# The w_out stage of a hybrid encoder step: norm row multiplied in as results leave PSUM, squares summed from PSUM, residual added in the last VectorE operation

## The chip, the cores and the metric

The kernel runs on one core of a Trainium2 chip. The metric is the device time of one execution in microseconds (us). Two times are told apart: the median of the timed runs, and the time of one execution that the hardware profiler recorded, from which all the rows of the profile come.

## The reference

One layer of a streaming encoder is computed for 2048 prompt rows and 128 sample rows (8 groups of 16), each row 1024 values wide, in float32. The stage that matters here is the third line: the two mixers' outputs are joined, multiplied by the 1024x1024 matrix `w_out`, normalised by the root mean square, scaled by a row of gains `norm_g[1]`, and added to the input.

```
att = rms_norm(att, g_att)                                  # 512 wide
mlstm_out = (hb * g_mlstm * sigmoid(ob))                    # 512 wide
x = x + rms_norm(concatenate([att, mlstm_out], -1) @ w_out, norm_g[1])
ffn, new_buf = conv_ffn(rms_norm(x, norm_g[2]), conv_buf, w_up, w_conv, b_conv, w_down)
x = x + rms_norm(ffn, norm_g[3])

def rms_norm(x, g):
    return x * rsqrt(mean(x * x, axis=-1, keepdims=True) + EPS) * g
```

The mean of squares is over the row before the gains are applied.

## The kernel before

The kernel is written with tiles and pools; a scheduler simulates the timeline when the kernel is built and puts each engine's instructions into an order from that. So a change in one place can move instructions on every engine near it.

The program has three large parts: the input projection with attention and mLSTM, the w_out stage, and the feed-forward part (an up projection, a short convolution, a gate, a down projection). Every matmul on large operands is done as three matmuls (`mm3`, L104 to L106) of pieces `hi` and `lo` of both factors: ScalarE makes `hi` by a cast and VectorE makes `lo` by subtracting `hi`. Splitting weights in the feed-forward part is done by L1309 (ScalarE) and L1310 (VectorE); combinations of weights are formed on VectorE in L1326.

The w_out stage is `project(tiles)` (L974 to L1040), a generator. It is advanced step by step, and between its steps other generators are advanced by a ratio of costs: at first the last attention heads (scores L394 and L395, transposes of the weights L76 into tile `pt`, their hi and lo pieces `pth` L417 and `ptl` L418, the product with the values L430 and L431 into `ot`), and from tile 8 on the first units of the feed-forward part (the rows of x are loaded as `x2r`, squared in L1095, scaled in L1099, transposed in L1107). The rows are taken in 17 tiles of 128 rows: tiles 0 to 7, then the sample tile (16), then tiles 8 to 15. For each tile:

- the joined row tile `mr` is loaded (two tiles ahead); for the next tile the attention half is normalised: a square with accumulation on ScalarE (L995), mean and inverse root on GpSimd (`rsqrt_mean`, L87 and L93), and the scaling on VectorE in L997;
- `turn_rows` transposes `mr` on TensorE (L76, PSUM tile `mT_pt`) and splits the result into the hi and lo pieces `mt` (L210 on ScalarE, L211 on VectorE). For tiles 0 to 7 this goes in two groups of four through the same PSUM buffers as the accumulators below (tag `mm`, two buffers); from the sample tile on through a larger buffer of its own (tag `big`);
- for each half `hf` of 512 columns 24 matmuls are accumulated in a PSUM tile `wo`. The half is evacuated by VectorE into `m` (L1026), and ScalarE squares it with accumulation (L1028); the squares themselves are written to a place that is free at that time and never read;
- the inverse root is formed on GpSimd (L87, L93), VectorE scales `m` by it and by the gains (L1038), GpSimd adds the residual row tile `xr` (L1039), and SyncE's queue stores the sum as `x2d` (L1040).

`m` and `xr` are the two halves of one tile `mx` (tag `wl`, two buffers); `xr` is loaded by SyncE's queue when the tile is begun (L1016). The slots of `wl` are used later for `wul`, the lo pieces of the first feed-forward weights. The gains lie in a tile of one buffer, `norm_row` (tag `grow`): row 1 is loaded ahead of the stage, and the row for the last norm of the layer takes its place after it (L98). There are 34 evacuations L1026, 34 squares L1028, and 17 each of L1038, L1039 and L1040. At the end of the kernel the last normalisation evacuates its PSUM tile with a product (L1691) and squares the same PSUM tile on ScalarE (L1692).

Of the kernel before, what the change touches and what calls it, by code (L numbers as in the profile page):

```python
# [12 lines left out]
AF = mybir.ActivationFunctionType  # L13
ALU = mybir.AluOpType
# [35 lines left out]
def hymba_step(ctx: ExitStack, tc: tile.TileContext, I: dict, O: dict):  # L50
    nc = tc.nc
# [8 lines left out]
    def ps_mm(name):  # L60
        return psum.tile([P, 512], F32, tag="mm", name=name)
# [24 lines left out]
    def mean_square(ms, ssq, n, eps=EPS):  # L86
        nc.gpsimd.tensor_scalar(ms, ssq, 1.0 / n, eps, op0=ALU.mult, op1=ALU.add)  # L87

    def rsqrt_mean(ssq, n, name, eps=EPS):
        ms = small.tile([P, 1], F32, tag="ms", name=name + "_ms")  # L90
        mean_square(ms, ssq, n, eps)
        rs = small.tile([P, 1], F32, tag="rs", name=name + "_rs")
        nc.gpsimd.tensor_tensor(rs, ms, nhalf[:, 0:1], op=ALU.pow)  # L93
        return rs
# [7 lines left out]
    def mm3(out, ah, al, bh, bl, start, stop, onto=False):  # L102

        nc.tensor.matmul(out, ah, bh, start=start, stop=False, skip_group_check=onto)  # L104
        nc.tensor.matmul(out, ah, bl, start=False, stop=False, skip_group_check=onto)  # L105
        nc.tensor.matmul(out, al, bh, start=False, stop=stop, skip_group_check=onto)  # L106
# [23 lines left out]
    def x_src(t):  # L130
        return I["x_sample"] if t == SAMPLE else I["x_prompt"][t * P:(t + 1) * P, :]
# [69 lines left out]
    def rows_to_T(hrow, chunk, j, name, bank):  # L201
        w = 4 if bank is not ps_big else KT
        for q in range(KT // w):
            pt = bank(f"{name}_pt{q}")
            for k in range(w):
                transpose(pt[:, k * P:(k + 1) * P], hrow[:, (w * q + k) * P:(w * q + k + 1) * P])
            ptv = pt.rearrange("p (k t) -> p k t", k=w)
            hv = chunk[:, 0, w * q:w * q + w, j * P:(j + 1) * P]
            lv = chunk[:, 1, w * q:w * q + w, j * P:(j + 1) * P]
            nc.scalar.copy(hv, ptv)  # L210
            nc.vector.tensor_tensor(lv, ptv, hv, op=ALU.subtract)  # L211
# [4 lines left out]
    def rows_tile(tag, shape, name, dtype=F32):  # L216
        if tag == "xr":
            return rows.tile(shape, dtype, tag="xr", name=name, bufs=2)
        return pa.tile(shape, dtype, tag=tag, name=name, bufs=1)
# [718 lines left out]
    g1 = []  # L938
# [31 lines left out]
    def drain():  # L970
        while any([p_.step() for p_ in pipes]):
            pass

    def project(tiles):  # L974

        ss = [SimpleNamespace(t=t) for t in tiles]

        def load(s):
            t = s.t
            if t == 8:  # L980
                drain()
                open_ffn()
            s.m = rows_tile("xr", [P, D], f"mr{t}")
            if t == SAMPLE:
                for b in range(DB):
                    own = bass.AP(atts[b].tensor, atts[b].offset, [[512, DS], [DS * 512 + DA, HA], [1, DA]])
                    nc.sync.dma_start(s.m[b * DS:(b + 1) * DS, 0:512].rearrange("p (h d) -> p h d", h=HA), own)
                nc.sync.dma_start(s.m[:, 512:D], mixs)
            else:
                nc.sync.dma_start(s.m, mixd[t // 4][:, t % 4, :])  # L990

        def norm(s):
            mt = wpool.tile([P, 2112], F32R, tag="wh", name=f"mt{s.t}", bufs=2)
            ssq = small.tile([P, 1], F32, tag="ssq", name=f"assq{s.t}")
            nc.scalar.activation(mt[:, :512], s.m[:, :512], AF.Square, accum_out=ssq)  # L995
            rs = rsqrt_mean(ssq, 512, f"att{s.t}")
            nc.vector.tensor_scalar(s.m[:, :512], s.m[:, :512], rs, None, op0=ALU.mult)  # L997
            s.mt = mt[:, :2 * D].rearrange("p (a k n) -> p a k n", a=2, k=KT)

        def turn_rows(s):  # L1000
            rows_to_T(s.m, s.mt, 0, f"mT{s.t}", ps_mm if s.t < 8 else ps_big)

        load(ss[0])
        norm(ss[0])
        yield 0.0, 0.3
        turn_rows(ss[0])
        load(ss[1])
        yield 0.9, 1.2
        for n_, s in enumerate(ss):
            t = s.t  # L1010
            nxt = ss[n_ + 1] if n_ + 1 < len(ss) else None
            if nxt:
                norm(nxt)
            mx = wpool.tile([P, 2112], F32, tag="wl", name=f"mx{t}", bufs=2)
            m, xr = mx[:, 0:D], mx[:, D:2 * D]
            nc.sync.dma_start(xr, x_src(t))  # L1016
            for hf in range(2):
                c = slice(hf * 512, hf * 512 + 512)
                acc = ps_mm(f"wo{t}_{hf}")
                for k in range(KT):  # L1020
                    mm3(acc, s.mt[:, 0, k, :], s.mt[:, 1, k, :], wo[k][0][:, c], wo[k][1][:, c],
                        start=(k == 0), stop=(k == KT - 1))
                    if k % 4 == 3:
                        yield 2.6, 0.5
                ssq = small.tile([P, 1], F32, tag="wssq", name=f"wssq{t}_{hf}")
                nc.vector.tensor_copy(m[:, c], acc)  # L1026
                idle = m[:, 512:D] if hf == 0 else s.mt[:, 0, 0:4, :].rearrange("p k n -> p (k n)")
                nc.scalar.activation(idle, m[:, c], AF.Square, accum_out=ssq)  # L1028
                if hf == 0:
                    ssa = ssq  # L1030
                    mean_square(ssa, ssq, D)
                    if nxt:
                        turn_rows(nxt)
                        if n_ + 2 < len(ss):
                            load(ss[n_ + 2])
                        yield 0.9, 1.2
            rs = rsqrt_mean(ssq, D, f"n1_{t}", ssa)
            nc.vector.scalar_tensor_tensor(m, m, rs, g1[0], op0=ALU.mult, op1=ALU.mult)  # L1038
            nc.gpsimd.tensor_tensor(xr, m, xr, op=ALU.add)  # L1039
            nc.sync.dma_start(x2d[t], xr)  # L1040


# [6 lines left out]
    def open_ffn():  # L1049

        p1.close()
        ffn.p3 = ctx.enter_context(tc.tile_pool(name="p3", bufs=2, reuse_waits="tile"))
        ffn.halo = ffn.p3.tile([P, 44, 2], F32, tag="halo", name="halo", bufs=1)
        nc.vector.memset(ffn.halo, 0.0)
        ffn.g2 = ffn.p3.tile([P, D], F32, tag="g2", name="g2", bufs=1)
        nc.sync.dma_start(ffn.g2, I["norm_g"][2:3, :].broadcast_to([P, D]))
        pipes[:] = [Pipe(h2_units(0, lead=6)), Pipe(iter([]))]
# [187 lines left out]
    for n_, (half, gi) in enumerate(seq):  # L1245
# [22 lines left out]
        if n_ == len(seq) - 1:  # L1268
            out = project([0, 1, 2, 3, 4, 5, 6, 7, SAMPLE, 8, 9, 10, 11, 12, 13, 14, 15])
            split = w_out_steps()  # L1270
            next(split)
            next(out)
# [194 lines left out]
    for b, tiles in enumerate(FBLOCKS):  # L1467
# [137 lines left out]
        for fi, f in enumerate(ORDERS[b]):  # L1605
# [12 lines left out]
            e, c = ec[:, 0:512], ec[:, 512:1024]  # L1618
# [193 lines left out]
        for dh in range(2):  # L1812
# [59 lines left out]
            for j in order:  # L1872
                if dh == 0:
                    half, ssq = out[j]
# [3 lines left out]
                else:  # L1878
                    half, ssq = out[j]
# [3 lines left out]
                    rs = p3.tile([P, 1], F32, tag=f"drs{j}", name=f"drs{tiles[j]}", bufs=2)  # L1883
# [104 lines left out]
```

## Time and profile before

| | |
|---|---|
| median of 3 runs | 2769.81 us (2767.66 to 2773.04) |
| profiled execution | 2768.79 us |
| its span | 2767.1 us |
| instructions | 47724 |
| TensorE busy | 2697.3 us, 97% of the span |
| VectorE busy | 1933.3 us, 70% |
| ScalarE busy | 1437.5 us, 52% |
| GpSimd busy | 674.8 us, 24% |

In the profile PE is TensorE's matmul, PEld its weight load, DVE is VectorE, ACT ScalarE, POOL GpSimd and SP SyncE, whose queue issues most transfers. `L1026` is line 1026 of the kernel. In a row of the trace, `mx<-wo` reads "written from", in square brackets stands how long the engine was idle before the instruction and what ended that, and `x17` is a count. The span runs from the first to the last recorded instruction; the time of the execution is 1.7 us longer here.

### The profile page before, as it was taken

Reading aid. Unit: us, or ns where it says so; the run is one execution under the profiler, and the core shown is the slowest. Engines: PE = TensorE matmul, PEld = TensorE weight load, DVE = VectorE, ACT = ScalarE, POOL = GpSimd, SP = SyncE. Lnnn points to the kernel's source line nnn. Section 1 sums busy time; section 2 is a strip of 40 time slices with the busy share of each in tenths; the row PEclk is TensorE's granted clock in tenths of the full one; section 3 lists DMA queues with packets and bytes.
Section 4 is the critical chain, followed back from the end, with each engine's and each line's share of the span. In section 5 each row is a group of like instructions: output and inputs, shape, how many; then the busy total and the mean of one; then the engine's idle time right before and its main releaser. Section 6 shows DMA issues by size and latency. Waiting matters only on the chain.

```text
span 2767.1 us, 47724 instructions
## 1 busy us (share of the span) xinstructions
PE 2697.3 (97%) x16422; PEld 2522.0 (91%) x16422; DVE 1933.3 (70%) x3593; ACT 1437.5 (52%) x2918; POOL 674.8 (24%) x1293
## 2 busy tenths in 40 slices
PE   8999999999999999999999999999999999999998
PEld 7899999999899998878999998789999878998976
DVE  5344455646446668766989988658888875998956
ACT  4355555635356666543555455444554665554554
POOL 1000010212100002334433322123343212556401
PEclk9999999999999999999999999999999999999999
DMA  5544355556564456345645559867886877788875
GB/s 186 156 120 137 104 164 167 160 154 213 161 183 142 137 168 197 109 165 196 231 152 188 167 179 331 296 225 203 245 239 182 252 236 242 220 263 239 253 262 178
DMA packets 329185, 539.72 MB, mean 195 GB/s; under 512 B 60354, under 2 KB 162974, under 8 KB 328814
## 3 DMA queue, kind: packets, MB, share of 16 engines
q1 hardware_dynamic: 248382, 393.82, 45.9%
q0 software_dynamic: 35632, 97.48, 11.4%
q10 hardware_dynamic: 44928, 45.37, 5.0%
q8 instruction: 129, 2.11, 0.3%
q14 instruction: 114, 0.93, 0.1%
HBM read 383.28 MB, written 162.68 MB: 197 GB/s over the span
## 4 chain that ended last, share of the span: by engine, by line
PE 51%; DVE 4%; DMA 2%; issue 1%; ACT 1%; POOL 1%; SPq 0%; DVEq 0%; POOLq 0%; ACTq 0%
PE uec L104 6%; PE uec L105 5%; PE uec L106 5%; PE dn L106 4%; PE dn L105 4%; PE dn L104 4%; PE ua L106 3%; PE ua L105 3%; PE ua L104 3%; PE dnm L105 2%; PE dnm L106 2%; PE dnm L104 2%; PE wo L106 2%; PE wo L104 2%; PE wo L105 1%
## 5 line engine op out<-in xcount | busy, mean ns | idle before, releaser
L104 PE MATMUL uec<-B,wuh 128*128 128x384 f32 (+1 forms) x720 | 236.3, 329 | 2.6 <-DVE uu L1646 2.6
L105 PE MATMUL uec<-B,wuh 128*128 128x384 f32 (+1 forms) x720 | 235.1, 327 | 0.0
L106 PE MATMUL uec<-B,wul 128*128 128x384 f32 (+1 forms) x720 | 233.7, 327 | 0.0
L1309 ACT CAST wuh<-wu 128x512 fp32r<-128x512 f32 x255 | 141.6, 618 | 107.4 <-PE uec L105 100.7
L1310 DVE TENSOR_TENSOR wul<-wu,wuh 128x512 fp32r<-128x512 f32 x255 | 165.0, 683 | 4.0 <-DMA x2d<-mx 2.8
L405 DVE CUSTOM_DVE_ANT_0 tmp<-s,nb 128x640 f32<-128x640 f32 (+4 forms) x128 | 94.3, 737 | 93.7 <-PE s L395 92.3
L104 PE MATMUL vo<-wi_h,hT 128*128 128x256 f32 x544 | 155.7, 286 | 0.6 <-DVE mt L211 0.6
L106 PE MATMUL vo<-wi_h,hT 128*128 128x256 f32 x544 | 156.2, 287 | 0.0
L105 PE MATMUL vo<-wi_l,hT 128*128 128x256 f32 x544 | 155.5, 286 | 0.0
L104 PEld LDWEIGHTS uec<-B,wuh 128*128 128x128 f32 x720 | 135.1, 188 | 6.1 <-DVE uu L1646 4.3
L105 PEld LDWEIGHTS uec<-B,wuh 128*128 128x128 f32 x720 | 135.3, 188 | 0.2
L106 PEld LDWEIGHTS uec<-B,wul 128*128 128x128 f32 x720 | 135.1, 188 | 0.0
L418 DVE TENSOR_TENSOR ptl<-pt,pth 128x640 fp32r<-128x640 f32 (+4 forms) x128 | 93.6, 737 | 57.7 <-ACT pth L417 56.7
L104 PE MATMUL qk<-hT,wi_h 128*128 128x384 f32 (+1 forms) x384 | 128.6, 335 | 5.0 <-ACT qk_st L236 3.9
L406 ACT ACTIVATE tmp<-tmp,mn 128x640 f32<-128x640 f32 (+4 forms) x128 | 97.6, 762 | 64.7 <-DVE mn L405 61.8
L1310 DVE TENSOR_TENSOR wdl<-wdr,wdh 128x512 fp32r<-128x512 f32 x198 | 125.0, 684 | 7.4 <-ACT wdh L1309 7.2
L1310 DVE TENSOR_TENSOR al<-ar,ah 128x768 fp32r<-128x768 f32 (+2 forms) x94 | 70.8, 763 | 82.1 <-ACT ah L1309 80.0
L105 PE MATMUL qb<-hT,wi_h 128*128 128x384 f32 (+1 forms) x384 | 127.9, 333 | 0.0
L105 PE MATMUL qk<-hT,wi_h 128*128 128x384 f32 (+1 forms) x384 | 127.6, 332 | 0.0
L106 PE MATMUL qk<-hT,wi_l 128*128 128x384 f32 (+1 forms) x384 | 127.3, 331 | 0.0
L106 PE MATMUL qb<-hT,wi_l 128*128 128x384 f32 (+1 forms) x384 | 127.2, 331 | 0.0
L104 PE MATMUL qb<-hT,wi_h 128*128 128x384 f32 (+1 forms) x384 | 127.2, 331 | 0.0
(448 smaller groups left out, 9404.0 us busy)
## 6 DMA issues: line engine op xcount, KB each, us to landing
wu<-in_w_up SPq DMA_DIRECT2D x220, 256.0 KB, 4.7
wu<-wsd SPq DMA_DIRECT2D x176, 256.0 KB, 4.5
wdr<-in_w_down SPq DMA_DIRECT2D x110, 256.0 KB, 5.2
wi_raw<-in_w_in SPq DMA_DIRECT2D x52, 512.0 KB, 4.0
wsd<-ws POOLq DMA_DIRECT2D x88, 256.0 KB, 3.5
wdr<-wtd SPq DMA_DIRECT2D x88, 256.0 KB, 5.1
gr<-gd SPq DMA_DIRECT2D x39, 384.0 KB, 5.9
kraw<-kTd SPq DMA_DIRECT2D x112, 128.0 KB, 3.5
```

The lines of the kernel that those rows point to most:

```text
L104: nc.tensor.matmul(out, ah, bh, start=start, stop=False, skip_group_check=onto)
L105: nc.tensor.matmul(out, ah, bl, start=False, stop=False, skip_group_check=onto)
L106: nc.tensor.matmul(out, al, bh, start=False, stop=stop, skip_group_check=onto)
L405: nc.vector.tensor_tensor_reduce(o_, s_, b_, 1.0, 3e38, ALU.add, ALU.min, accum_out=mn)
L406: nc.scalar.activation(tmp[:, :n], tmp[:, :n], AF.Exp, bias=mn, scale=-1.0, accum_out=rsum[:, i % 4, hh:hh + 1])
L418: nc.vector.tensor_tensor(s.ptl[:, sl, qc], ptv, s.pth[:, sl, qc], op=ALU.subtract)
L1309: nc.scalar.copy(h, r)
L1310: nc.vector.tensor_tensor(l, r, h, op=ALU.subtract)
```

## The change

The evacuation of each half multiplies by the gains instead of copying. The squares are taken from the PSUM accumulator, since `m` now holds the product with the gains, and the mean of squares must be taken before it. The last VectorE operation multiplies `m` by the inverse root and adds the residual row in the place of the gains, and writes into `xr`. The addition on GpSimd is gone. One line fewer makes every later line of the changed kernel one lower, so that L1310 and L1326 are there L1309 and L1325.

```
                 ssq = small.tile([P, 1], F32, tag="wssq", name=f"wssq{t}_{hf}")
-                nc.vector.tensor_copy(m[:, c], acc)
+                nc.vector.tensor_tensor(m[:, c], acc, g1[0][:, c], op=ALU.mult)
                 idle = m[:, 512:D] if hf == 0 else s.mt[:, 0, 0:4, :].rearrange("p k n -> p (k n)")
-                nc.scalar.activation(idle, m[:, c], AF.Square, accum_out=ssq)
+                nc.scalar.activation(idle, acc, AF.Square, accum_out=ssq)
...
             rs = rsqrt_mean(ssq, D, f"n1_{t}", ssa)
-            nc.vector.scalar_tensor_tensor(m, m, rs, g1[0], op0=ALU.mult, op1=ALU.mult)
-            nc.gpsimd.tensor_tensor(xr, m, xr, op=ALU.add)
+            nc.vector.scalar_tensor_tensor(xr, m, rs, xr, op0=ALU.mult, op1=ALU.add)
             nc.sync.dma_start(x2d[t], xr)
```

The order of instructions differs from before only in a stretch of each engine's queue from the w_out stage to the start of the feed-forward part; ahead of it and behind it the rows are the same. Three places are shown.

GpSimd between the end of tile 6 and the end of tile 7, before (`n_6` are the mean and inverse root of a w_out row, `att` those of the attention half of the next tile, `wssq` a sum of squares of one half):

```order
L87 TENSOR_SCALAR n_6_ms<-wssq_1_15073,wssq_0_14960 128x1
L93 TENSOR_TENSOR n_6_rs<-n_6_ms,nhalf 128x1
L87 TENSOR_SCALAR att_ms<-assq_15084 128x1
L93 TENSOR_TENSOR att_rs<-att_ms,nhalf 128x1
L1039 TENSOR_TENSOR mx_14881<-mx_14881 128x1024
L87 TENSOR_SCALAR wssq_0_15144<-wssq_0_15144 128x1
L87 TENSOR_SCALAR n_7_ms<-wssq_1_15196,wssq_0_15144 128x1
```

The same place of the same engine in the changed kernel:

```order
L87 TENSOR_SCALAR n_6_ms<-wssq_1_15067,wssq_0_14954 128x1
L93 TENSOR_TENSOR n_6_rs<-n_6_ms,nhalf 128x1
L87 TENSOR_SCALAR att_ms<-assq_15077 128x1
L93 TENSOR_TENSOR att_rs<-att_ms,nhalf 128x1
L87 TENSOR_SCALAR wssq_0_15137<-wssq_0_15137 128x1
L87 TENSOR_SCALAR n_7_ms<-wssq_1_15189,wssq_0_15137 128x1
```

The addition of 128x1024 that stood between the inverse root for the next tile's attention half and the mean of squares of the next half is gone; nothing has taken its place.

TensorE where the transposes of tile 7 stand among the last attention heads, before, with the semaphores that each instruction waits on (`mT_pt` are the two groups of transposes, `s` is a score tile):

```order
L76 MATMUL mT_pt_14964<-ident,mr_14800 128x128 [waits DMAHW6_49,DVE_49]
L76 MATMUL mT_pt_14964<-ident,mr_14800 128x128 x3
L76 MATMUL mT_pt_14971<-ident,mr_14800 128x128 [waits DVE_49]
L76 MATMUL mT_pt_14971<-ident,mr_14800 128x128 x3
L394 MATMUL s_14_14988<-kh_3_14572,qs_3_14574 128x320 [waits DVE_49]
```

The same place in the changed kernel:

```order
L76 MATMUL mT_pt_14958<-ident,mr_14795 128x128 [waits DMAHW6_49,DVE_49]
L76 MATMUL mT_pt_14958<-ident,mr_14795 128x128 x3
L76 MATMUL mT_pt_14965<-ident,mr_14795 128x128 [waits Activation_49]
L76 MATMUL mT_pt_14965<-ident,mr_14795 128x128 x3
L394 MATMUL s_14_14982<-kh_3_14568,qs_3_14570 128x320 [waits DVE_49]
```

The order is the same, but the second group waits for ScalarE where it waited for VectorE: its buffer was last read by the squares and no longer by the copy.

SyncE at the start of the feed-forward part, before (`wu` are weights of the up projection, `wcv` and `sext` constants of the convolution):

```order
L1453 DMA wcv<-in_w_conv 128x176
L1455 DMA sext<-in_cache_conv 128x704
L1321 DMA wu_0_16384<-in_w_up 128x512
L1321 DMA wu_1_16386<-in_w_up 128x512
L98 DMA norm_row_16220<-in_norm_g 128x1024
L1040 DMA x2d_295<-mx_16095 128x1024
L1321 DMA wu_2_16388<-in_w_up 128x512
L1321 DMA wu_3_16390<-in_w_up 128x512
```

The same eight rows of the changed kernel:

```order
L98 DMA norm_row_16203<-in_norm_g 128x1024
L1452 DMA wcv<-in_w_conv 128x176
L1454 DMA sext<-in_cache_conv 128x704
L1320 DMA wu_0_16367<-in_w_up 128x512
L1320 DMA wu_1_16369<-in_w_up 128x512
L1320 DMA wu_2_16371<-in_w_up 128x512
L1039 DMA x2d_295<-mx_16079 128x1024
L1320 DMA wu_3_16373<-in_w_up 128x512
```

The load of the gains for the last norm stands ahead of the constants and of two loads of weights that were ahead of it, and the last store of a w_out row stands behind one more load of weights. On VectorE, at the same place of the program, three combinations of weights (L1326) that stood behind the last evacuation L1026 now stand ahead of it.

## The prediction

> **What bounds the kernel now.** I read the page first, then the busy time by stage, then what TensorE waits for in the stage that the change touches, and last the instructions around those waits in order of time.
>
> ```profile
> PE 2697.3 (97%) x16422; PEld 2522.0 (91%) x16422; DVE 1933.3 (70%) x3593; ACT 1437.5 (52%) x2918; POOL 674.8 (24%) x1293
> ```
>
> TensorE is busy for 97% of the span, so work that leaves VectorE, ScalarE or GpSimd is worth nothing in itself. It is worth only what TensorE waited for it. The next view gives the busy time of each engine before, in, and after the stretch in which the w_out outputs leave PSUM (columns: length, PE, PEld, DVE, ACT, POOL, clock, DMA).
>
> ```profile
> 0.00:1060.00 1060.00, 1024.08 (x7358) 995.17 (x7359) 580.10 (x1423) 552.42 (x1318) 94.75 (x291) 1.00 0.53 158
> 1060.00:1340.00 280.00, 273.18 (x1466) 231.33 (x1465) 204.55 (x306) 135.26 (x310) 107.89 (x143) 1.00 0.52 171
> 1340.00:2767.00 1427.00, 1400.04 (x7602) 1295.45 (x7600) 1148.66 (x1867) 749.80 (x1291) 472.15 (x859) 0.99 0.73 227
> ```
>
> In the 280 us from 1060 to 1340 TensorE is idle for 280.00 - 273.18 = 6.8 us. That is nearly all that this change can win, since its 34 evacuations all lie there and the first TensorE row that it moves lies there too. The clock is full. Which waits make up the 6.8 us is told by TensorE's waits in this window (engine, line, what it waited for: total us, times, longest).
>
> ```profile
> PE pt L76 <- DVE ptl L418: 1.8, 1, 1.8
> PE ua L106 <- DVE wul L1310: 1.6, 1, 1.6
> PE h2T_pt L1107 <- DVE x2r L1099: 0.9, 1, 0.9
> PE wo L106 <- DVE mt L211: 0.7, 2, 0.4
> PE ot L431 <- DVE ptl L418: 0.5, 1, 0.5
> PE wo L104 <- DVE mt L211: 0.4, 1, 0.4
> PE s L394 <- DVE ptl L418: 0.3, 1, 0.3
> PE ub L106 <- DVE wu L1310: 0.2, 1, 0.2
> ```
>
> Every one of the nine waits is for VectorE, 6.4 us in all, though VectorE is busy for only 204.55 of 280 us. So VectorE is late at certain moments, and the question is why. The operations on tile mx (min/median/max ns) and on line 997 show it.
>
> ```profile
> L1026 DVE COPY mx<-wo x34: 674/680/692, 1060.1 to 1317.9; 128x512 f32<-128x512 f32 x34
> L1028 ACT ACTIVATE mx<-mx x17: 620/632/636, 1060.8 to 1312.2; 128x512 f32<-128x512 f32 x17
> L1028 ACT ACTIVATION_READ_ACCUMULATOR mx<-mx x17: 185/187/192, 1061.3 to 1312.7; 128x1 f32 x17
> L1028 ACT ACTIVATE mt<-mx x17: 622/632/648, 1069.0 to 1318.7; 128x512 fp32r<-128x512 f32 x17
> L1028 ACT ACTIVATION_READ_ACCUMULATOR mt<-mx x17: 185/187/204, 1069.5 to 1319.2; 128x1 f32 x17
> L1038 DVE SCALAR_TENSOR_TENSOR mx<-mx,n_rs,norm_row x17: 1268/1284/1286, 1070.8 to 1321.5; 128x1024 f32<-128x1024 f32 x17
> L1039 POOL TENSOR_TENSOR mx<-mx x17: 2374/2396/2578, 1072.7 to 1323.1; 128x1024 f32<-128x1024 f32 x17
> ```
> ```profile
> L997 DVE TENSOR_SCALAR mr<-mr,att_rs x17: 477/2604/2624, 1009.1 to 1298.0; 128x512 f32<-128x512 f32 x17
> ```
>
> One and the same VectorE instruction, L997, takes 0.48 us at its best and 2.60 us in the median. The order of time, around the longest wait, says when it is slow.
>
> ```profile
> 1170.93 2.40 POOL L1039 TENSOR_TENSOR mx<-mx 128x1024 f32<-128x1024 f32 x1
> 1171.00 2.62 DVE L997 TENSOR_SCALAR mr<-mr,att_rs 128x512 f32<-128x512 f32 x1 [0.71 <-POOL att_rs L93]
> ...
> 1174.30 0.63 ACT L1028 ACTIVATE mx<-mx 128x512 f32<-128x512 f32 x1 [5.63 <-POOL mx L1039]
> ```
> ```profile
> 1175.66 0.31 PE L394 MATMUL s<-kh,qs 128*128 128x320 f32 x1
> 1175.81 0.31 PE L395 MATMUL s<-kl,qs 128*128 128x320 f32 x1
> 1177.94 0.77 PE L76 MATMUL pt<-ident,tmp 128*128 128x128 f32 x5 [1.82 <-DVE ptl L418]
> ```
>
> GpSimd's residual add runs from 1170.93 to 1173.33, and L997, started beside it, ends at 1173.62, 0.29 us after it. It is held for the whole add and loses 2.62 - 0.48 = 2.1 us. The copy L1026 of the next tile stands behind L997 on VectorE. The sum of squares L1028 needs that copy and holds ScalarE's queue for 5.63 us until 1174.30. The attention's hi and lo pieces (L417, L418) come behind both, and TensorE stops for 1.82 us.
>
> **What the change does, part by part.** The sum is made against the profiled execution, 2768.8 us for a span of 2767.1; the median of the three timed runs, 2769.8, is 1.0 us above it.
>
> The copy L1026 becomes a product of PSUM and the norm row, and L1028 reads PSUM. The same pair stands already at the end of the kernel, as L1691 and L1692, on the same shapes:
>
> ```profile
> 2758.20 0.69 DVE L1691 TENSOR_TENSOR last<-dn,norm_row 128x512 f32<-128x512 f32 x1 [5.30 <-PE dn L106]
> 2758.93 0.60 ACT L1692 ACTIVATE junk<-dn 128x512 f32<-128x512 f32 x1 [8.31 <-DVE last L1691]
> ```
>
> So the product costs 0.69 us for the copy's 0.68: 34 times 0.01, or 0.3 us of VectorE, which has 75 us free in this stage; nothing. The squares cost 0.60 for 0.63: nothing. They also don't start earlier: L1692, which reads the same PSUM tile as L1691, begins only after it (2758.20 + 0.69 = 2758.89). In the changed order L1028 still waits for VectorE. What is new is that the accumulator is held longer: by the product, the squares and the read of the accumulator, 0.69 + 0.60 + 0.19 = 1.48 us, where the copy alone held it for 0.68. For tiles 0 to 7 the next user of that bank can be the second group of transposes mT_pt, which now waits for ScalarE. The Trainium skill, "PSUM — Partial Sum Buffer", section "PSUM bank collisions raise a hardware error", speaks against this part: two engines may not access one bank and quadrant at a time, reads included, so a scheduler puts a dependency between them. The tail rows agree with it; by it the hold is 1.48 us, without it 0.79 at most and the charge made below would be nothing.
>
> What does the hold cost? Below, it could be nothing: the copy now comes up to 2.1 us earlier where L997 is no longer held, more than the added 0.80 us. Above, eight tiles by 0.80 is 6.4 us. No row of TensorE's waits names the copy, so I take it near the low end, and put 1.0 us for it and for the moved rows of TensorE together; both ends go into the range.
>
> The scale and gain (L1038) keep their shape, 1.28 us, with x in place of the norm row as the second tensor; nothing. x was loaded for the add anyway, and VectorE instead of GpSimd now waits for it; its load is issued about two tiles ahead, so I put nothing. Were x late, L997 and the next tile's product would stand behind this wait on VectorE. The norm row was loaded before the stage began.
>
> On SyncE's queue, the load of the feed-forward part's norm row (L98) moves ahead of two weight loads. It takes the place of the old norm row and so waits for that row's last reader, now the last L1026.
>
> ```profile
> 1320.48 0.96 SPq L1321 DMA_DIRECT2D wu<-in_w_up  x2
> 1322.79 0.33 SPq L98 DMA_DIRECT2D norm_row<-in_norm_g  x1
> ```
>
> The last L1026 began at 1317.9; in the changed order three of the 0.68 us combinations of line 1326 stand newly ahead of it, so it ends by 1317.9 + 3 x 0.69 + 0.69 = 1320.7 at the latest, and the weights behind L98 leave at most 0.6 us later than their 1320.48, or earlier if VectorE is ahead by then. I take nothing.
>
> The add L1039 goes: 17 x 2.40 = 41 us of GpSimd. What counts is whom it held. This row groups L997 in the stage (busy, mean):
>
> ```profile
> L997 DVE TENSOR_SCALAR mr<-mr,att_rs 128x512 f32<-128x512 f32 x15 | 32.8, 2185 | 8.7 <-POOL att_rs L93 8.7
> ```
>
> VectorE wins 15 x (2.185 - 0.477) = 26 us, in pieces of 2.1 us at just the moments at which the copy, and behind it ScalarE, are waited for. Now the waits one by one. The 1.8 us wait for ptl shrinks by up to 2.1: gone, 1.8. The two others for ptl, 0.8 together, lie behind L997 in the same way: gone. The three for mt (1.1): VectorE's lateness makes part of them, the rest is the plain chain transpose, cast, subtract; I take 0.7. The wait for x2r comes from ScalarE:
>
> ```profile
> 1209.35 0.63 ACT L1028 ACTIVATE mx<-mx 128x512 f32<-128x512 f32 x1 [5.64 <-POOL mx L1039]
> ...
> 1215.48 0.63 PE L1107 MATMUL h2T_pt<-ident,x2r 128*128 128x128 f32 x4 [0.91 <-DVE x2r L1099]
> ```
>
> The squares of x2r stand behind this L1028 on ScalarE; 2.1 us earlier covers 0.91: gone, 0.9. Late next is the load of x2r. Last, the turn into the feed-forward part:
>
> ```profile
> 1314.92 0.69 DVE L1310 TENSOR_TENSOR wul<-wu,wuh 128x512 fp32r<-128x512 f32 x1 [2.83 <-DMA x2d<-mx]
> ...
> 1323.13 2.51 POOL L1039 TENSOR_TENSOR mx<-mx 128x1024 f32<-128x1024 f32 x1
> ...
> 1323.75 2.45 DVE L1310 TENSOR_TENSOR wu<-ws,wu 128x512 fp32r<-128x512 f32 x1
> ```
>
> The first weight split waits for the store of a w_out row, which now leaves 2.4 us earlier, and a later split is held by the last add, 2.45 where its kind takes 0.69. VectorE gains some 1.8 to 4 us ahead of the waits of ua and ub: both gone, 1.8. Sum: 1.8 + 0.8 + 0.7 + 0.9 + 1.8 = 6.0 us.
>
> A stop costs more than the idle time that is recorded, since records overlap: above, neighbouring matmuls start 0.15 us apart and the stop takes 2.13 from start to start, so 1.98 is lost where 1.82 is shown. With 0.16 for each of some eight stops, 1.2 more. Less the 1.0 charged: 6.0 + 1.2 - 1.0 = 6.2 us, so 2762.6 for a profiled execution and 2763.6 for the median.
>
> **Rivals.** *Forecast (0.58):* TensorE gets most of its waits back, 2763.6, its own range 2760 to 2764.3.
>
> *The relief arrives, but other waits come first (0.33):* the scheduler has moved rows on every engine up to the start of the feed-forward part, and TensorE, running earlier, meets the next late thing (the load of x2r, the chain through the transposes, the split of the first weights). For it: the three waits for mt have a part that nothing here touches. Against: what it meets is mostly VectorE's, which is 2.1 us earlier. If half of 7.2 comes back and 1.0 is charged, 2.6 us: 2767.2, no change by measure.
>
> *The PSUM bank becomes the wait (0.09):* the squares queue on ScalarE behind casts, and the bank of an accumulator comes free only after them. Each of 34 holds is 0.80 us longer; if all were on TensorE's path that is 27 us. It decides for slower from (7.2 + 5.5) / 0.80 = 16 of the 34 on. With 17 of them: 13.6 - 7.2 = 6.4 slower, 2776.2. Against it: only tiles 0 to 7 give the bank to transposes at once; the later ones have another half tile of matmuls in between.
>
> *The change doesn't shorten the chain as its words suggest:* that the squares run beside the evacuation is already refused by the tail rows, and is priced at nothing.
>
> **How the numbers follow.** About 0.2%, 5.5 us, is what a measurement of this kernel can tell from no change (its three runs lie 5.4 apart). The forecast lies just beyond it, so faster has 0.58, within 0.33, slower 0.09. Low end: all 6.4 and nine stops of 0.16, 7.8, nothing charged, and 2 us for the runs' spread: 2760. The high end takes in the second case with as much spread: 2769. Slower is left out.
>
> **What would show it.** In the profile after: no L1039; L997 at 0.48 us throughout; the ScalarE wait ahead of L1028 shorter by about 2 us; L1026 at 0.69 and L1028 at 0.60; TensorE's idle time from 1060 to 1340 near 1 to 2 us, with the 1.8 and 1.6 gone. It is wrong if L997 stays near 2.6 us (then the add was not what held it), if TensorE waits for L1028 by name at mT_pt, or if the idle time stays near 6 us under other names.

## The result, and the profile after

The changed kernel takes 2764.93 us in the median of 22 runs (2757.26 to 2770.04) where the kernel before took 2769.47 in as many beside it: 4.5 us less, a ratio of 0.9981 with a 95% interval of 0.9973 to 0.9988. In a second measurement the ratio was 0.9985 (0.9976 to 0.9994). It is faster, but only about as far from no change as the 0.2% that the prediction set as its bound. The median lies between the forecast (6.2 us less) and its second case (2.6 less); the first interval, 3.3 to 7.5 us less, takes in the forecast and not the second case.

The page's busy times, and the stage from 1060 to 1340 us (columns as before: length, PE, PEld, DVE, ACT, POOL, clock, DMA):

```profile
PE 2692.4 (97%) x16422; PEld 2520.0 (91%) x16422; DVE 1902.5 (69%) x3593; ACT 1437.1 (52%) x2918; POOL 627.4 (23%) x1276
```
```profile
1060.00:1340.00 280.00, 276.51 (x1497) 235.73 (x1496) 176.82 (x314) 138.63 (x320) 65.77 (x126) 1.00 0.52 172
```

TensorE is idle for 3.5 us there, where it was 6.8 and the prediction expected 1 to 2. VectorE has 27.7 us less to do (204.55 before). What TensorE still waits for in this window:

```profile
PE wo L106 <- DVE mt L211: 1.2, 3, 0.5
PE pt L76 <- DVE ptl L418: 0.6, 1, 0.6
PE s L394 <- DVE ptl L418: 0.5, 1, 0.5
PE mT_pt L76 <- DVE mt L211: 0.4, 1, 0.4
PE h2T_pt L1106 <- DVE x2r L1098: 0.4, 1, 0.4
PE ot L430 <- ACT pth L417: 0.3, 1, 0.3
```

The wait for the first weights (1.6 for wul) is gone, the longest one has shrunk from 1.8 to 0.6, and the waits for mt have not shrunk at all. The operations on mx and line 997:

```profile
L1026 DVE TENSOR_TENSOR mx<-wo,norm_row x34: 676/691/692, 1064.7 to 1321.6; 128x512 f32<-128x512 f32 x34
L1028 ACT ACTIVATE mx<-wo x17: 597/599/605, 1065.4 to 1314.4; 128x512 f32<-128x512 f32 x17
L1038 DVE SCALAR_TENSOR_TENSOR mx<-mx,n_rs x17: 1269/1285/1287, 1076.5 to 1325.1; 128x1024 f32<-128x1024 f32 x17
```
```profile
L997 DVE TENSOR_SCALAR mr<-mr,att_rs x17: 478/486/490, 1013.9 to 1299.5; 128x512 f32<-128x512 f32 x17
```

Line 997 takes 0.49 us every time now. The place of the longest wait, in order of time:

```profile
1172.20 1.29 DVE L1038 SCALAR_TENSOR_TENSOR mx<-mx,n_rs 128x1024 f32<-128x1024 f32 x1 [0.78 <-POOL n_rs L93]
1172.25 1.29 POOL L87 TENSOR_SCALAR att_ms<-assq 128x1 f32<-128x1 f32 x1
1173.62 0.56 POOL L93 TENSOR_TENSOR att_rs<-att_ms,nhalf 128x1 f32<-128x1 f32 x1
1174.22 0.49 DVE L997 TENSOR_SCALAR mr<-mr,att_rs 128x512 f32<-128x512 f32 x1 [0.73 <-POOL att_rs L93]
1175.63 0.69 DVE L1026 TENSOR_TENSOR mx<-wo,norm_row 128x512 f32<-128x512 f32 x1 [0.93 <-PE wo L106]
1176.41 0.60 ACT L1028 ACTIVATE mx<-wo 128x512 f32<-128x512 f32 x1 [4.50 <-issue]
```

VectorE now waits 0.93 us for the matmul before it can evacuate: it is ahead of TensorE and no longer behind. The squares begin at 1176.41, when the product that reads the same accumulator ends (1175.63 + 0.69 = 1176.32), and ScalarE has stood 4.50 us at its queue's head, where it was 5.63.

The parts of the program ahead of the stage and behind it differ by some us from profile to profile, though no instruction there stands elsewhere. So the stretch between two fixed rows is compared: the first w_out matmul, and the first matmul of line 104 of the down projection that reads ah. Before, a second profile of before, and after (minimum, median and maximum in ns, then the first and last start in us):

```profile
L104 PE MATMUL wo<-wo,mt x272: 390/396/497, 1049.2 to 1316.1; 128*128 128x512 f32 x136
L104 PE MATMUL dn<-wdh,ah x308: 387/390/628, 2159.0 to 2757.3; 128*128 128x512 f32 x154
```
```profile
L104 PE MATMUL wo<-wo,mt x272: 389/396/505, 1052.7 to 1319.3; 128*128 128x512 f32 x136
L104 PE MATMUL dn<-wdh,ah x308: 387/393/629, 2160.9 to 2760.6; 128*128 128x512 f32 x154
```
```profile
L104 PE MATMUL wo<-wo,mt x272: 389/396/502, 1053.9 to 1318.3; 128*128 128x512 f32 x136
L104 PE MATMUL dn<-wdh,ah x308: 387/393/628, 2157.8 to 2752.4; 128*128 128x512 f32 x154
```

Before: 2159.0 - 1049.2 = 1109.8 and 1108.2 us. After: 1103.9, and 1103.2 in its second profile. Between these profiles the change shortens this stretch by 4.3 to 6.6 us, so the gain lies there. Two profiles of one kernel differ by up to 1.6 us in it.

### The profile page after: what moved, and what is told of

It reads as the page before. It is cut to its first block, busy times and chain, and to the rows that moved or that the text cites. A ratio compares the mean times of both kernels' runs of the same rounds, so it can differ in the third digit from the quotient of the medians.

```text
span 2762.2 us, 47713 instructions
## 1 busy us (share of the span) xinstructions
PE 2692.4 (97%) x16422; PEld 2520.0 (91%) x16422; DVE 1902.5 (69%) x3593; ACT 1437.1 (52%) x2918; POOL 627.4 (23%) x1276
## 4 chain that ended last, share of the span: by engine, by line
PE 79%; DMA 10%; DVE 5%; ACT 2%; issue 2%; POOL 1%; SPq 0%; ACTq 0%; DVEq 0%; POOLq 0%
PE uec L104 6%; PE uec L105 6%; PE uec L106 6%; PE dn L106 4%; PE dn L104 4%; PE dn L105 4%; PE ua L106 3%; PE ua L105 3%; PE ua L104 3%; PE qb L105 2%; PE qb L106 2%; PE qb L104 2%; PE pt L76 2%; PE wo L106 2%; PE wo L105 2%
## 5 line engine op out<-in xcount | busy, mean ns | idle before, releaser
L1309 DVE TENSOR_TENSOR wul<-wu,wuh 128x512 fp32r<-128x512 f32 x255 | 165.1, 683 | 3.7 <-DMA x2d<-mx 2.3
L1309 DVE TENSOR_TENSOR wdl<-wdr,wdh 128x512 fp32r<-128x512 f32 x198 | 125.0, 685 | 7.8 <-ACT wdh L1308 7.6
L106 PE MATMUL dn<-wdh,al 128*128 128x512 f32 x308 | 124.1, 403 | 2.6 <-DVE al L1309 2.6
```

The source lines that it names most:

```text
L1309: nc.vector.tensor_tensor(l, r, h, op=ALU.subtract)
```

## The experiments

All times are against the kernel before, run beside each. Idle is TensorE's from 1060 to 1340; stretch is the one just described. Both come from one profile each. Against itself the kernel before came out 1.8 us shorter in the median (8 runs against 9), with an interval from 0.23% less to 0.17% more: a difference of that size says nothing alone.

| kernel | median against before, us | ratio (95%) | idle, us | stretch, us |
|---|---|---|---|---|
| before, two profiles; the second against before | -1.8 | 0.9997 (0.9977 to 1.0017) | 6.8, 6.9 | 1109.8, 1108.2 |
| changed, twice | -4.5, -4.3 | 0.9981 (0.9973 to 0.9988), 0.9985 (0.9976 to 0.9994) | 3.5, 2.9 | 1103.9, 1103.2 |
| unread add, on two chips | +2.0, +1.3 | 1.0007 (0.9998 to 1.0015), 1.0011 (1.0002 to 1.0019) | 7.9, 7.1 | 1113.1, 1111.7 |
| unread half add | -3.0 | 0.9987 (0.9977 to 0.9997) | 4.2 | 1108.3 |
| unread add in four pieces | -3.6 | 0.9985 (0.9974 to 0.9996) | 6.2 | 1109.9 |
| unread add, last tile | -3.7 | 0.9985 (0.9976 to 0.9995) | 3.9 | 1103.8 |
| unread add, tiles 4 and 5 | -2.3 | 0.9994 (0.9982 to 1.0005) | 3.9 | 1106.7 |
| before, L997 on ScalarE | -0.8 | 0.9994 (0.9981 to 1.0007) | 5.2 | 1106.7 |
| before, squares from PSUM | +5.7 | 1.0016 (1.0006 to 1.0025) | 8.1 | 1113.5 |
| changed, squares from SBUF | +0.7 | 0.9999 (0.9989 to 1.0009) | 5.7 | 1107.8 |
| before, add moved, gains left out | +9.2 | 1.0035 (1.0022 to 1.0049) | 5.3 | 1116.3 |

**Putting the add back.** The theory was that GpSimd's add, by holding VectorE, is what TensorE paid for. Its rivals: the row that is stored earlier, the squares and the product, or the order of instructions. An add that nobody reads and for which the store doesn't wait brings back the hold, and with it only the time on GpSimd's own queue, and the scheduler leaves the order as in the changed kernel but for a handful of rows of TensorE, VectorE and ScalarE.

```
             nc.vector.scalar_tensor_tensor(xr, m, rs, xr, op0=ALU.mult, op1=ALU.add)
+            nc.gpsimd.tensor_tensor(m, m, xr, op=ALU.add)
             nc.sync.dma_start(x2d[t], xr)
```

> The changed kernel with a GpSimd add of the same shape put back behind the last VectorE operation, whose result nobody reads and for which the store doesn't wait. The hold theory: L997 goes back to 2.6 us and nearly all of the gain is lost: TensorE's idle time from 1060 to 1340 back to 6 to 8 us, time within 1.5 us of before. If instead the gain came from the store that leaves a step earlier, or from the squares and the product, the time stays at the changed kernel's, 4.5 us below before.

Line 997 is held again and the stops stand where they were (line 997, and TensorE's waits):

```profile
L997 DVE TENSOR_SCALAR mr<-mr,att_rs x17: 478/2606/2644, 1010.2 to 1300.2; 128x512 f32<-128x512 f32 x17
```
```profile
PE ua L106 <- DVE wul L1310: 2.0, 1, 2.0
PE pt L76 <- DVE ptl L418: 1.6, 1, 1.6
PE ot L430 <- ACT pth L417: 1.2, 1, 1.2
```

The whole gain is lost, and in the medians 1.3 to 2.0 us more. Repeated beside kernels with a part of the adds, it came out the same:

> The changed kernel with the unread add behind all 17 tiles once more, on the chip of the two kernels with a part of the adds. The hold theory: 4 to 8 us above the changed kernel and so 0 to 4 us above before, with stops at the same places as in its first run; the two partial kernels lie between. If its first time came from its chip, it is within 2 us of the changed kernel.

So the add costs some 6 us against the changed kernel (2.0 + 4.5 and 1.3 + 4.3, each a difference of two differences from before). The earlier store and the cheaper chain don't carry the gain, since both are as in the changed kernel here. The rest of the change, order included, wins nothing that these runs show; whether it costs 1 or 2 us is not settled, since the first interval takes in no change.

**Half of it, and four pieces.** The same line with 128x512, and with four operations of 128x256:

> The changed kernel with a GpSimd add of half the size (128x512) behind the last VectorE operation, whose result nobody reads; TensorE's order differs from the changed kernel's in 4 rows. The hold theory: L997 near 1.4 us, between 0.49 without and 2.6 with the whole add, and the time between the changed kernel's and that with the whole add, some 2 to 5 us above the changed kernel. If it is not the length of the hold but the mere presence of an add that moves the order, the time is that with the whole add, 5 to 7 us above the changed kernel.

> The changed kernel with the whole unread add in four GpSimd operations of 128x256. If VectorE's held instruction gets its turn when the running piece ends, L997 takes 0.5 to 1.3 us and the time stays within 3 us of the changed kernel. If GpSimd's next piece starts ahead of it each time, L997 takes 2.6 us or more and the time is that with the whole add, 5 to 7 us above the changed kernel.

With half, line 997 takes 1.50 us in the median. With four pieces, the place of the longest wait looks like this (GpSimd's x4 is one row for the four):

```profile
1173.36 3.01 POOL L1041 TENSOR_TENSOR mx<-mx 128x256 f32<-128x256 f32 x4
1173.43 0.96 DVE L997 TENSOR_SCALAR mr<-mr,att_rs 128x512 f32<-128x512 f32 x1 [0.72 <-POOL att_rs L93]
1174.71 0.69 DVE L1026 TENSOR_TENSOR mx<-wo,norm_row 128x512 f32<-128x512 f32 x1 [0.33 <-PE wo L106]
```

A piece takes 0.74 us in the median, and line 997 is done 0.96 after its start: it gets its turn when the first piece ends. The product, which has one operand in PSUM, keeps its 0.69 us beside the later pieces. The Trainium skill's page "SBUF — State Buffer", section "Who interferes with whom", states this: the pair of ports that VectorE shares with GpSimd is locked for a whole instruction, and a VectorE instruction with at most one SBUF input, outside the two-port modes, doesn't take it. The trace agrees on both points.

The pieces also tell the hold from the other thing that an add does, which is to occupy GpSimd's own queue: here they occupy it for 3.01 us, longer than the whole add's 2.40, and in time the pieces cost nothing that 12 runs can tell (-3.6). Half the add came out near the changed kernel too (-3.0 for -4.3); the midway that was expected, about -1.4, lies inside its interval (6.4 to 0.8 us less), so it is neither shown nor refused.

Pieces don't help everywhere. At the last tile VectorE has four operations in a row that read two SBUF tiles, the combinations of B:

```profile
L1041 POOL TENSOR_TENSOR mx<-mx x68: 721/737/2259, 1078.3 to 1331.1; 128x256 f32<-128x256 f32 x68
1325.92 7.39 POOL L1041 TENSOR_TENSOR mx<-mx 128x256 f32<-128x256 f32 x4 [1.40 <-DVE mx L1038]
1326.23 8.71 DVE L1168 TENSOR_TENSOR B<-B 128x1536 fp32r<-128x1536 f32 x4
```

Taken singly, pieces and combinations end by turns there (pieces at 1326.67, 1328.89, 1331.10 and 1333.32, combinations at 1328.29, 1330.50, 1332.72 and 1334.93), each held by the other: the last three pieces take 2.26 us each, and the four combinations together 8.71, as long as with one whole add (8.73, below). From there comes this kernel's stop of 2.3 us ahead of the up projection, and with it most of what its idle time (6.2) has over the changed kernel's 3.5. With half the add the combinations take 7.62 us and that stop is 0.8.

**Which holds cost what.** The whole unread add, behind the last tile only and behind tiles 4 and 5 only:

```
+            if t == 15:            # in the other kernel: t in (4, 5)
+                nc.gpsimd.tensor_tensor(m, m, xr, op=ALU.add)
```

> The changed kernel with the unread GpSimd add of 128x1024 behind the last of the 17 tiles only; every engine's order but for that one row on GpSimd is the changed kernel's. The hold theory, with the prediction's 1.8 us for the two waits at the turn into the feed-forward part: VectorE's four combinations of the tile B that stand beside the add take about 8.7 us where they take 6.8 in the changed kernel, TensorE's wait for wul by the up projection's L106 comes back with 1.6 to 2.0 us, nothing changes ahead of it, and the time is 1.5 to 3.5 us above the changed kernel. If that wait came from the late store of the row, which this kernel doesn't delay, it stays gone and the time is the changed kernel's.

TensorE's first wait, and VectorE and GpSimd at the last tile, with the add:

```profile
PE ua L106 <- DVE wul L1311: 1.7, 1, 1.7
```
```profile
1326.72 2.41 POOL L1040 TENSOR_TENSOR mx<-mx 128x1024 f32<-128x1024 f32 x1 [1.40 <-DVE mx L1038]
...
1327.02 8.73 DVE L1167 TENSOR_TENSOR B<-B 128x1536 fp32r<-128x1536 f32 x4
```

The same four combinations in the changed kernel:

```profile
1326.80 6.75 DVE L1165 TENSOR_TENSOR B<-B 128x1536 fp32r<-128x1536 f32 x4
```

The first combination of B waits for the add, 8.73 - 6.75 = 1.98 us, the weights' lo piece stands behind it, and TensorE stops for 1.7. But for this one row, every engine's order is that of the changed kernel, so the stop is the hold of this one add and not the late store. From the last w_out matmul of line 104 to the first down-projection matmul that reads gh this profile takes 1641.8 - 1318.5 = 323.3 us, where the two of the changed kernel take 1639.9 - 1318.3 = 321.6 and 321.7: the stop is all there. The long stretch (1103.8) hides it, since the part ahead is about as much shorter in this one profile, and in the median it is lost in the spread (-3.7).

> The changed kernel with the unread GpSimd add behind tiles 4 and 5 only, the two ahead of the stops at 1155 to 1160 and 1176 in the kernel before. The hold theory as the prediction had it: the stops of 1.8 and 0.8 us come back, TensorE loses 2.5 to 3 us more between 1150 and 1185 than in the changed kernel, and the time is about that much above it. If the order that the scheduler gave the changed kernel took away part of them, 1 us or less comes back.

The wait for ptl is back with 1.6 us, as with all the adds, so these two adds made 1.0 us of it in the changed order; 0.6 is there without them. The time lies between, but its interval takes in no change.

**L997 on ScalarE, with the add left in place:**

```
-            nc.vector.tensor_scalar(s.m[:, :512], s.m[:, :512], rs, None, op0=ALU.mult)
+            nc.scalar.activation(s.m[:, :512], s.m[:, :512], AF.Copy, scale=rs)
```

> The kernel before with the scaling L997 put on ScalarE, with the add left on GpSimd. The hold theory: nothing long stands in VectorE's queue beside the add any more, the copy L1026 of the next tile comes up to 2.1 us earlier, and 3 to 5 us of the time are won, TensorE's idle time from 1060 to 1340 near 4 us. If the later end of the add and of the store was what cost the time, it stays within 1.5 us of before. Against a gain stands ScalarE's own queue: L997 takes about 0.65 us there and stands ahead of the squares.

Idle goes to 5.2 us and the median moves by 0.8 only, less than the 3 to 5 expected; the interval (5.3 us less to 1.9 more) settles neither. TensorE's waits in that profile show what is left: the feed-forward waits that the last add makes, 1.6 and 0.6 us, and 2.5 us for ptl. On ScalarE, which also runs the squares, line 997 takes 0.73 us, and the order moved as well, so this kernel tests the hold less cleanly than the unread add.

```profile
PE ua L106 <- DVE wul L1310: 1.6, 1, 1.6
PE s L394 <- DVE ptl L418: 1.5, 1, 1.5
PE pt L76 <- DVE ptl L418: 0.8, 1, 0.8
PE ub L106 <- DVE wu L1310: 0.6, 1, 0.6
```

**One part at a time.** The kernel before with the squares alone taken from PSUM (`m[:, c]` becomes `acc` in the activation), and the changed kernel with the squares alone put back on SBUF (the reverse):

> The kernel before with only the squares taken from the PSUM accumulator. The hold theory: no gain, L997 stays near 2.6 us, TensorE's idle time from 1060 to 1340 stays between 6 and 9 us, time within 0 to +2 us of before (the longer hold of the accumulator). If the squares run beside the copy and shorten the chain, L1028 begins with the copy and not 0.7 us after it, and 1 to 3 us are won.

> The changed kernel with the squares taken from the product rows in SBUF and no longer from the PSUM accumulator, so that the accumulator is free after the product; the squares then hold the gains, which is not the reference's mean. If the longer hold of the accumulator costs the 1.0 us that the prediction charged, this one is about 1 us faster than the changed kernel, and TensorE's second group of transposes waits for VectorE again; if it costs nothing, the two agree within 1.5 us apart from what the order at tile 2 does, where some 90 rows of TensorE differ.

Both lose. With squares from PSUM alone the adds still hold line 997 (2.61 us), and the squares begin 0.76 us after the copy does, as in the kernel before:

```profile
1177.65 0.68 DVE L1026 COPY mx<-wo 128x512 f32<-128x512 f32 x1
1178.41 0.60 ACT L1028 ACTIVATE mx<-wo 128x512 f32<-128x512 f32 x1 [5.60 <-POOL mx L1039]
```

This kernel loses 5.7 us where 0 to 2 were expected. Its profile shows stops that before hasn't, 1.5 us ahead of line 430 and 0.6 for a tile `ad`, and none that names the squares; how much of the 5.7 is the longer hold of the accumulator and how much the moved order stays open.

With squares back on SBUF the accumulator is free earlier, yet the kernel loses all of the gain. TensorE's longest wait, and ScalarE ahead of it:

```profile
PE ot L430 <- ACT pth L417: 3.9, 1, 3.9
```
```profile
1081.42 0.42 ACT L660 ACTIVATE mvo<-mvo 128x256 f32<-128x256 f32 x1 [2.98 <-DMA mvo<-vobd]
1081.75 0.61 ACT L1028 ACTIVATE mx<-mx 128x512 f32<-128x512 f32 x1
...
1082.94 1.25 ACT L417 CAST pth<-pt 128x640 fp32r<-128x640 f32 x2
```

Here the scheduler has put L660, which waits 2.98 us for a load, and the squares ahead of the cast L417. In the changed kernel the same three stand the other way round:

```profile
1081.52 1.29 ACT L417 CAST pth<-pt 128x640 fp32r<-128x640 f32 x2 [0.47 <-PE ot L430]
...
1083.70 0.41 ACT L660 ACTIVATE mvo<-mvo 128x256 f32<-128x256 f32 x1
...
1084.62 0.60 ACT L1028 ACTIVATE mx<-wo 128x512 f32<-128x512 f32 x1
```

So no wait shows the longer hold of the accumulator, but since the order moved in both kernels, neither rules out that it costs something. A choice of order at one place, a stop of 3.9 us for 0.3, is worth more than half of what all the adds cost.

The last of the kind moves only the add and leaves the gains out:

```
-            nc.vector.scalar_tensor_tensor(m, m, rs, g1[0], op0=ALU.mult, op1=ALU.mult)
-            nc.gpsimd.tensor_tensor(xr, m, xr, op=ALU.add)
+            nc.vector.scalar_tensor_tensor(xr, m, rs, xr, op0=ALU.mult, op1=ALU.add)
```

> The kernel before with only the residual moved into the last VectorE operation; the evacuation stays a copy, the squares stay on the copied rows, and the gains of the row are left out of the result. If the hold of VectorE by GpSimd's add was what TensorE paid for, all of the gain is here: L997 near 0.49 us throughout, TensorE's idle time from 1060 to 1340 near 3.5 us or below (before 6.8, the changed kernel 3.5), time 4 to 6 us below before. If the longer hold of the PSUM accumulator by the squares costs something in the changed kernel, this one is faster than the changed kernel by that, 1 us by the prediction. If the gain came from the squares or the product, this one stays within 1.5 us of before.

Line 997 is down to 0.49 us, and yet this kernel is 9.2 us slower. It has the same stop ahead of line 430 (3.1 us). Besides, nothing reads the row of gains any more, so the load of the next row (L98), which before leaves at 1322.8 us, leaves at 552.0, and the order changed as far as the middle of the feed-forward part; the stretch is 6.5 us longer than before. It says nothing clean on the add.

**The controls.** The changed kernel and the kernel before once more:

> The changed kernel once more, on the chip of the three kernels that go with it, since the first four experiments ran on a chip where the kernel before took 3 us longer. Expected: 2 to 7 us below before, L997 near 0.49 us, TensorE's idle time from 1060 to 1340 near 3.5 us. If the first four experiments lost time to that chip and not to their own order of instructions, this kernel too shows the stop of 1.2 to 3.1 us ahead of line 430 at tile 2, where ScalarE's cast L417 comes late; if it was their order, it does not.

> The kernel before once more, for a second profile of it. The changed kernel's two profiles begin the w_out stage 4.7 and 6.0 us later than the one profile of before, though no instruction stands in another place until then, and are 3.4 to 3.7 us shorter behind the feed-forward part's first down projection of the late half, where the order is the same again. If this is variation between executions, the first w_out matmul lies anywhere between 1047 and 1056 us here; if the changed kernel itself does it, it lies within 1 us of 1049.2. In both cases the stretch from the first w_out matmul to the first down-projection matmul of ah is near 1109.8 us, against 1103.9 and 1103.2 in the changed kernel, with TensorE's stops of 1.8 and 1.6 us in place.

The changed kernel has the short wait of 0.3 us ahead of line 430 again. The unread add has 1.2 us there on both of its chips, and on the second of them the kernels with a part of the adds have 0.3: the stop belongs to the kernel's order and not to a chip. The second profile of before repeats the first one's stops to the tenth (1.8 for ptl, 1.6 for wul, 0.9 for x2r), and its first w_out matmul starts at 1052.7: that start differs by 3.5 us between two profiles of one kernel, while these three stops in the stage do not.

## Why the prediction was right, and where it was not

**The cause** was right: the add holds line 997, 2.61 us with a whole add, 1.50 with half, 0.95 with four pieces, 0.49 without, and the unread add alone takes the whole gain back while the same work in pieces doesn't. The prices of product and squares were right to 0.01 us, and so was the step that the squares don't run beside the evacuation.

**The waits** were mis-sized: 6.0 of 6.4 us were to go, 3.0 went (6.4 to 3.4; 2.9 left in the second profile). Item by item: *ptl*, 1.8 + 0.8 predicted gone, 1.1 stays. Tiles 4 and 5 show that the hold's part of the 1.8 was about 1.0 to 1.2; the rest stays without any add: it is the chain that makes ptl, a cast and a subtraction, which is late next. *mt*, 0.7 predicted gone, but 1.1 became 1.6. One wait went (0.4 at 1160 us) and two came, 0.4 at 1066 and 0.5 at 1308. The second has a place, shown after and then before:

```profile
1297.67 1.64 SPq L1320 DMA_DIRECT2D wu<-in_w_up  x3
1299.36 0.42 SPq L1039 DMA_DIRECT2D x2d<-mx  x1
1304.38 0.69 DVE L1325 TENSOR_TENSOR ws<-wu,wu 128x512 f32<-128x512 f32 x1 [2.90 <-DMA wu<-in_w_up]
...
1306.91 1.22 DVE L211 TENSOR_TENSOR mt<-mT_pt,mt 128x1024 fp32r<-128x1024 f32 x1
```
```profile
1296.21 1.65 SPq L1321 DMA_DIRECT2D wu<-in_w_up  x3
1300.39 0.33 SPq L1040 DMA_DIRECT2D x2d<-mx  x1
1302.08 0.69 DVE L1326 TENSOR_TENSOR ws<-wu,wu 128x512 f32<-128x512 f32 x1 [0.83 <-DMA wu<-in_w_up]
```

L211 stands behind four combinations of weights in both, but in the changed kernel their weights land later: the first combination begins 1304.38 - 1299.31 = 5.07 us after the last of their loads was issued, where it was 1302.08 - 1297.86 = 4.22 (4.91 and 4.09 in the second profiles). The store of the finished row, which no longer waits for the add, is issued right behind these loads and not 2.5 us later, so its transfer can overlap theirs; that this delays them is likely, but no run tests it. The prediction counted the earlier store as a gain alone, and had looked at SyncE's queue only at L98, which comes after this place. *x2r*: 0.9 predicted gone, 0.4 left in one profile and none named in the other. *ua and ub*: 1.8 predicted gone, and gone. The prediction gave two reasons for them, the late store and a held split L1310. With the last add alone put back the wul wait returns although the store is early, and what is held in the changed order is the combination of B.

**The added cost of a stop** (1.2 for eight stops) looks too small: idle time fell by 3.3 to 4.0 us, the stretch by 4.3 to 6.6. That each stop costs more than it shows fits this, but the stretch also takes in work behind the window, and no run prices a single stop.

**The charge of 1.0** was put mostly on the longer hold of the accumulator. No wait of TensorE names the squares, and the kernel without that hold is not faster, though its order differs. With the unread add put back the kernel lies 1.3 to 2.0 us above before in the medians, so the whole charge may have been near right or somewhat small. That the sum of 6.2 came near the measured 4.5 is in part luck: the waits, its largest term, gave half of what was counted, and what made up for it is not separated here.

**Of the rivals**, the bank hold did not show. The second one, relief that meets other waits, describes what is left: of the 3.4 us, 1.6 are for mt and 1.1 for ptl, which is the chain through the transposes that it named, and one of these waits stands behind weights that land late.

**Smaller points.** ScalarE's wait ahead of L1028 shrank by 1.1 us, not 2, since the product now waits for the matmul. The weights behind L98 left later than the 0.6 us allowed: 1323.88 in the profile after, against 1320.48, when that part of the program ran 2.2 us later (last w_out matmul 1318.3 against 1316.1). No wait of TensorE followed.

## What to carry to other kernels

An elementwise operation on GpSimd that is off the critical path is not free where VectorE, released by the same chain, starts an SBUF operation beside it: look for one VectorE line whose minimum and median differ by nearly the GpSimd operation's length, and count what queues behind it. Fold such an operation into a VectorE one that runs anyway. Cutting it into pieces frees a single held operation after the first piece, but not a row of them, since each next piece holds the next one again. Under a scheduler that orders by a simulated timeline, test a part by adding an unread operation to the finished version, whose order then nearly stays, and not by building the part alone: taking a part out moved the order here, and one such move made a stop of 3.9 us.

## What the runs showed of the hardware that was not expected

The hold works both ways, and it catches the smallest operation. In the lines above from 1172.20, GpSimd's L87 on 128x1 takes 1.29 us and ends as L1038 does, where the same line, also on 128x1, takes 0.27 a microsecond earlier, with L1038 not yet running:

```profile
1171.26 0.27 POOL L87 TENSOR_SCALAR n_ms<-wssq,wssq 128x1 f32<-128x1 f32 x1 [3.34 <-ACT mt L1028]
```

This was so before, too: the row of L87 for the attention half takes 1.28 us in the median before and 1.29 after, and 0.19 at its best. So the add's removal freed VectorE, and VectorE's own last operation still holds GpSimd's chain by about 1 us in most tiles; no wait of TensorE names that chain here.
